# Result tiles turned in 32 by 32 blocks by VectorE, and stored in runs of 128 bytes

## The chip, the cores and the metric

One core of one Trainium2 chip runs the whole program. The time is device microseconds for one execution. Engines named here: TensorE (PE, with its weight loads PEld), VectorE (DVE), ScalarE (ACT), GpSimd (POOL) and SyncE (SP). SyncE does no arithmetic: it issues DMA transfers, one after the other, each once the semaphores that it waits for have come.

## The reference

A residual block on x of 512 tokens by 1024 features, one layer, in float32: a SwiGLU feed-forward network at half weight, a mixer (gated DeltaNet heads and latent attention heads), and a second such network. Each has adaptive layer normalisation from a conditioning vector c.

```
for l in range(DEPTH):
    mod = sc @ w_ada[l] + b_ada[l]
    sh1, s1, g1, sh2, s2, g2, sh3, s3, g3 = jnp.split(mod, N_MOD, axis=-1)
    h = _modulate(x, sh1, s1)
    x = x + 0.5 * g1[:, None, :] * _swiglu(h, ffn1_w_in[l], ffn1_w_out[l])
    h = _modulate(x, sh2, s2)
    y = _hybrid_mixer(h, cos, sin, ...)
    x = x + g2[:, None, :] * y
    h = _modulate(x, sh3, s3)
    x = x + 0.5 * g3[:, None, :] * _swiglu(h, ffn2_w_in[l], ffn2_w_out[l])
return x
```

The change is in how the last x leaves the chip. The output has a row for each token: 1024 floats, 4096 bytes.

## The kernel before

x is kept turned: `self.xT[t]`, t = 0 to 7, is a tile of 128 partitions (features 128t to 128t+127) by 512 columns (tokens). Matrix products are done in three passes of a high and a low part (`mm3`, lines 280 to 282), so that one product of 128 features by 512 tokens is three matmuls.

The second feed-forward network ends in `ffn_pairs`. Its down projection is summed by groups of four blocks of the hidden width; each group updates xT at once. The last group has six blocks. For output tile t, `steps_of(t, a, b, ts)` issues the matmuls of blocks a to b into the PSUM tile `ends[t]`, and `finish(t, ts, p)` (line 990) is VectorE's update: xT[t] becomes p times the gate, plus xT[t]. `close` does this for tiles 0 to 3, whose updates come one behind the other, and returns `leave2`, which ends the kernel with tiles 4 to 7. Tile 7 is done in two halves of 256 tokens, both in one PSUM tile, so that the end has less behind it. A full tile is 18 matmuls.

Each tile of xT must be turned back, since the output has tokens as rows. `store(t, blocks)` does it: for each block of 128 tokens TensorE makes a transpose of 128 by 128 into a PSUM tile (line 731), ScalarE copies the PSUM tile to SBUF (line 733), and SyncE issues one DMA (line 128, the helper `load`) that writes runs of 128 floats, 512 bytes, one for each token. In `leave2` the stores of tiles 0 to 5 go in pairs between the matmuls of tiles 4, 5 and 6 and their updates; that of tile 6 comes between the halves of tile 7; tile 7's own store is in two halves at the very end.

The order of the work in this stretch is the order of the program: `in_order` ties every instruction to the one before it on its engine. Buffers `o` come from a ring of 56 slots of 128 by 512 floats; as many are taken after as before. Two other places of this kernel have operations of the kinds that the change brings in: `base_blocks` (lines 1634 to 1658) sends small matrices through DRAM, in runs of 128 and 64 bytes, some from all 128 partitions and some from 64, and `inverse` (lines 1676 and 1687) makes VectorE transposes in blocks of 32 by 32.

Of the kernel before, what the change touches and what calls it, by code (L numbers as in the profile page):

```python
# [18 lines left out]
P = 128  # L19
# [3 lines left out]
NB = NT // P  # L23
# [66 lines left out]
class Block:  # L90
# [632 lines left out]
            waiting = g  # L723
        next(waiting, None)

    def store(self, t, blocks):
        nc = self.nc
        b0, n = blocks[0], len(blocks)
        p = self.aux()
        for i, b in enumerate(blocks):  # L730
            nc.tensor.transpose(p[:, i * P:(i + 1) * P], self.xT[t][:, b * P:(b + 1) * P], self.ident)
        o = self.slot(s="o")
        nc.scalar.copy(o[:, :n * P], p[:, :n * P])
        self.load(self.out[0][b0 * P:(b0 + n) * P, t * P:(t + 1) * P].rearrange("(b p) n -> p b n", p=P),
                  o[:, :n * P].rearrange("p (b n) -> p b n", b=n))

    def ffn2(self, nb):
        ins = self.ins
# [203 lines left out]
    def ffn_pairs(self, w1, w2, gate, plain, raws, split, accs, side=None):  # L942

        nc = self.nc
        full = slice(0, NT)
        tasks, fill = {}, {}
        add = lambda at, go: tasks.setdefault(at, []).append(go)
        n = FT - plain
# [29 lines left out]
        if side:  # L978
            for i, k in enumerate((0, 4, 1, 5, 2, 6, 3, 7)):
                t = self.token_sums(k % 4, k // 4, True)  # L980
# [8 lines left out]
        def finish(t, ts, p):  # L989
            nc.vector.scalar_tensor_tensor(out=self.xT[t][:, ts], in0=p[:, ts], scalar=gate()[:, t:t + 1],  # L990
                                           in1=self.xT[t][:, ts], op0=ALU.mult, op1=ALU.add)
# [74 lines left out]
        def steps_of(t, a, b, ts=full):  # L1066
            if t not in ends:
                ends[t] = self.aux() if t in ((3, 6, 7) if side else (3,)) else self.acc()
            self.dense(ends[t], units[t][1:], self.act[k0:], ts, a, b, m - 1)
# [3 lines left out]
        for t, s in enumerate((stop, stop + 2, stop + 4, stop + 6)):  # L1073
            add(s, lambda t=t: unit_hi(t))
            add(s + 1, lambda t=t: unit_lo(t))
        last = {stop + 2: (0, 0, 2), stop + 4: (0, 2, 4), stop + 5: (1, 0, 2), stop + 7: (1, 2, 4), stop + 8: (2, 0, 2),
                stop + 10: (2, 2, 4), stop + 11: (0, 4, 5)}
# [72 lines left out]
            return self.norm_half(1, accum, 3)  # L1150

        def leave2():
            for t in range(4, KT - 1):
                steps_of(t, 0, m)
                for e in range(2 * t - 8, min(2 * t - 6, t)):
                    self.store(e, range(NB))
                finish(t, full, ends[t])
            t = KT - 1
            ends[t] = self.acc()
            for half in range(2):  # L1160
                ts = slice(half * HALF, half * HALF + HALF)
                steps_of(t, 0, m, ts)
                finish(t, ts, ends[t])
                if half == 0:
                    self.store(t - 1, range(NB))
                else:
                    self.store(t, range(2))
            self.store(t, range(2, 4))

        return close  # L1170

# [1093 lines left out]
```

## Time and profile before

| | us |
|---|---|
| median of 3 runs | 1039.08 (1038.6 to 1039.15) |
| the profiled execution | 1038.9 |
| its span, first to last instruction | 1037.2 |
| TensorE busy | 1019.9 (98% of the span) |
| VectorE busy | 757.8 (73%) |
| ScalarE busy | 484.2 (47%) |
| DMA, mean over the span | 135 GB/s |

The span is that of one profiled execution; the run takes a little longer than the span. Busy times of TensorE are of pipelined matmuls, so neighbours overlap, and spacing from start to start tells more than the length of one. Times in the rows count from the start of the span. A DMA's row on SPq is the time that its issue takes on SyncE, not that of the transfer. The granted clock of TensorE is 0.999 of full speed over the span.

### The profile page before, as it was taken

To read this page: it belongs to the slowest core of one execution; us is meant where nothing else is said; L and a number is where in the kernel's file an instruction comes from. 1 tells how busy PE (TensorE), PEld (TensorE's weight loads), DVE (VectorE), ACT (ScalarE), POOL (GpSimd) and SP (SyncE) were. 2 spreads that over 40 slices of the span, in tenths; PEclk is the share of its full clock that TensorE was granted. 3 is DMA by queue.
4 is the path that set the end of the run, shared out by engine and by line. 5 is a ranking of instruction groups with operands and counts; after the bars stand their busy time and mean duration, and the time that the engine had idled before them with its cause. 6 is when DMAs were issued, how large, how long until landed. Compare 5 with 4: busy or idle time off the path is not lost.

```text
span 1037.2 us, 17073 instructions
## 1 busy us (share of the span) xinstructions
PE 1019.9 (98%) x6673; PEld 889.2 (86%) x6673; DVE 757.8 (73%) x1416; ACT 484.2 (47%) x865; POOL 114.2 (11%) x232
## 2 busy tenths in 40 slices
PE   7999999999999999999999999999999999999998
PEld 5787878889998999888868778998999999999987
DVE  4467988888887876648977656788778778777642
ACT  4342233255544355649566463565445444444431
POOL 0033331222120101100001111310000000000000
PEclk9999999999999999999999999999999999999999
DMA  9987876778785348511311211163423424323222
GB/s 276 291 269 237 284 225 220 223 191 223 206 216 129 90 106 209 142 41 42 101 41 36 73 42 42 34 150 102 143 82 103 122 82 123 101 82 116 68 61 82
DMA packets 187278, 140.21 MB, mean 135 GB/s; under 512 B 14385, under 2 KB 176190, under 8 KB 187198
## 3 DMA queue, kind: packets, MB, share of 16 engines
q1 hardware_dynamic: 175646, 100.33, 33.9%
q0 software_dynamic: 11552, 38.81, 13.7%
q8 instruction: 52, 0.85, 0.3%
q14 instruction: 28, 0.23, 0.1%
HBM read 127.18 MB, written 2.49 MB: 125 GB/s over the span
## 4 chain that ended last, share of the span: by engine, by line
PE 84%; issue 5%; DVE 4%; ACT 2%; DMA 2%; POOL 1%; SPq 0%; POOLq 0%; DVEq 0%; ACTq 0%
PE pa L280 14%; PE pa L281 13%; PE pa L282 13%; PE pb L916 9%; PE pb L914 9%; PE pb L915 9%; PE pb L280 3%; PE pb L282 2%; PE pb L281 2%; POOL ar L579 1%; PE pb L435 1%; PE pb L1597 1%; DMA wl<-wr 1%; PE pb L1998 1%; PE pb L2028 1%
## 5 line engine op out<-in xcount | busy, mean ns | idle before, releaser
L280 PE MATMUL pa<-ah,wh 128*128 128x512 f32 (+1 forms) x346 | 133.1, 385 | 0.7 <-DVE xT L990 0.5
L281 PE MATMUL pa<-al,wh 128*128 128x512 f32 (+1 forms) x346 | 132.6, 383 | 0.0
L282 PE MATMUL pa<-ah,wl 128*128 128x512 f32 (+1 forms) x346 | 130.9, 378 | 0.2 <-DVE wl L1064 0.2
L280 PE MATMUL pa<-hh,wh 128*128 128x512 f32 (+1 forms) x293 | 110.2, 376 | 0.5 <-ACT hh L482 0.4
L281 PE MATMUL pa<-hl,wh 128*128 128x512 f32 (+1 forms) x293 | 109.2, 373 | 0.6 <-DVE hl L474 0.3
L282 PE MATMUL pa<-hh,wl 128*128 128x512 f32 (+1 forms) x293 | 108.2, 369 | 0.0
L990 DVE SCALAR_TENSOR_TENSOR xT<-pa,mod,xT 128x512 f32<-128x512 f32 (+1 forms) x79 | 57.2, 727 | 37.7 <-PE pa L282 37.7
L579 POOL DMA_DIRECT2D ar<-in_w_ada x112 | 63.4, 635 | 153.3 <-DVE aa L590 46.2
L282 PEld LDWEIGHTS pa<-ah,wl 128*128 128x128 f32 x346 | 65.1, 188 | 13.4 <-DVE wl L1064 0.6
L590 DVE SCALAR_TENSOR_TENSOR aa<-ar,sc,aa 128x512 f32<-128x512 f32 x98 | 73.2, 747 | 2.2 <-DMA ar<-in_w_ada 0.8
L280 PEld LDWEIGHTS pa<-ah,wh 128*128 128x128 f32 x346 | 65.8, 190 | 6.7 <-DVE xT L990 1.1
L281 PEld LDWEIGHTS pa<-al,wh 128*128 128x128 f32 x346 | 65.8, 190 | 5.5 <-DVE al L875 0.2
L280 PEld LDWEIGHTS pa<-hh,wh 128*128 128x128 f32 x293 | 55.3, 189 | 13.0 <-issue 3.4
L208 DVE TENSOR_TENSOR wl<-wr,wh 128x1024 fp32r<-128x1024 f32 (+1 forms) x33 | 38.4, 1164 | 35.7 <-ACT wh L203 35.4
L914 PE MATMUL pb<-fh,wh 128*128 128x256 f32 x224 | 63.4, 283 | 0.5 <-ACT cc L850 0.5
L916 PE MATMUL pb<-hh,wl 128*128 128x256 f32 x224 | 63.4, 283 | 0.2 <-DMA wl<-wr 0.2
L282 PEld LDWEIGHTS pa<-hh,wl 128*128 128x128 f32 x293 | 55.3, 189 | 9.6 <-DVE wl L208 0.4
L281 PEld LDWEIGHTS pa<-hl,wh 128*128 128x128 f32 x293 | 55.3, 189 | 9.3 <-DVE hl L474 1.2
L916 PE MATMUL pb<-fh,wl 128*128 128x256 f32 x224 | 63.3, 283 | 0.0
L915 PE MATMUL pb<-fl,wh 128*128 128x256 f32 x224 | 63.2, 282 | 0.0
L915 PE MATMUL pb<-hl,wh 128*128 128x256 f32 x224 | 63.2, 282 | 0.0
L914 PE MATMUL pb<-hh,wh 128*128 128x256 f32 x224 | 63.2, 282 | 0.0
(448 smaller groups left out, 2793.9 us busy)
## 6 DMA issues: line engine op xcount, KB each, us to landing
wr<-in_ffn_w_in SPq DMA_DIRECT2D x82, 512.0 KB, 3.9
ar<-in_w_ada POOLq DMA_DIRECT2D x112, 256.0 KB, 5.2
wr<-in_ffn_w_out SPq DMA_DIRECT2D x32, 512.0 KB, 5.0
wr<-in_w_in SPq DMA_DIRECT2D x21, 512.0 KB, 3.7
wl<-wr POOLq DMA_DIRECT2D x18, 512.0 KB, 5.7
ar<-in_w_ada SPq DMA_DIRECT2D x16, 512.0 KB, 8.2
wr<-in_ffn_w_out SPq DMA_DIRECT2D x16, 384.0 KB, 4.8
wr<-in_w_out SPq DMA_DIRECT2D x8, 512.0 KB, 3.4
```

What stands on the lines that cost most here:

```text
L208: self.nc.vector.tensor_tensor(out=lo, in0=raw, in1=hi.bitcast(F32), op=ALU.subtract)
L280: mm(out, wh, xh, start=start, stop=False)
L281: mm(out, wh, xl, start=False, stop=False)
L282: mm(out, wl, xh, start=False, stop=stop)
L435: nc.tensor.matmul(pg[32 * q:32 * q + 32, :256], self.sc[:, kc:kc + 1].to_broadcast([P, 32]), a[:, kc], start=(e == 0), stop=(e == 1), til ...
L579: nc.gpsimd.dma_start(tiles[i], a1[kc * P:(kc + 1) * P, o:o + NT])
L590: nc.vector.scalar_tensor_tensor(out=acc, in0=a, scalar=sc, in1=acc, op0=ALU.mult, op1=ALU.add)
L914: mm(out, wh, xh, start=start and k == 0, stop=False, **kw)
L915: mm(out, wh, xl, start=False, stop=False, **kw)
L916: mm(out, wl, xh, start=False, stop=stop and k == 3, **kw)
L990: nc.vector.scalar_tensor_tensor(out=self.xT[t][:, ts], in0=p[:, ts], scalar=gate()[:, t:t + 1], in1=self.xT[t][:, ts], op0=ALU.mult, op1= ...
L1597: nc.tensor.matmul(pa[:, ps], kh[:, ps], x[:, ps], start=True, stop=True)
```

## The change

`store` no longer uses TensorE, PSUM and ScalarE. VectorE transposes the tile (or half tile) in blocks of 32 by 32: within each group of 32 partitions, block j of 32 columns is turned in place. Partition 32i + a of `o` then holds, for each j, feature 32i to 32i + 31 of token 32j + a. So four DMAs are issued, one for each i, each from 32 partitions; they write runs of 32 floats, 128 bytes, 16 runs from each partition for a full tile and 8 for a half. For the last half tile two of the four are issued on ScalarE's queue instead of SyncE's. The stores of tiles 0 to 3 now stand together at the start of `leave2`, each other tile's right behind its update, and there are no transposes left between the matmuls.

```diff
-    def store(self, t, blocks):
-        nc = self.nc
-        b0, n = blocks[0], len(blocks)
-        p = self.aux()
-        for i, b in enumerate(blocks):
-            nc.tensor.transpose(p[:, i * P:(i + 1) * P], self.xT[t][:, b * P:(b + 1) * P], self.ident)
+    def store(self, t, ts, last=False):
+
+        nc = self.nc
+        w = ts.stop - ts.start
         o = self.slot(s="o")
-        nc.scalar.copy(o[:, :n * P], p[:, :n * P])
-        self.load(self.out[0][b0 * P:(b0 + n) * P, t * P:(t + 1) * P].rearrange("(b p) n -> p b n", p=P),
-                  o[:, :n * P].rearrange("p (b n) -> p b n", b=n))
+        nc.vector.transpose(out=o[:, :w], in_=self.xT[t][:, ts])
+        dst = self.out[0][ts, t * P:(t + 1) * P].rearrange("(j a) n -> a j n", a=32)
+        for i in range(4):
+            queue = nc.scalar if last and i % 2 else nc.sync
+            queue.dma_start(dst[:, :, 32 * i:32 * i + 32], o[32 * i:32 * i + 32, :w].rearrange("a (j b) -> a j b", b=32))
...
         def leave2():
+            for e in range(4):
+                self.store(e, full)
             for t in range(4, KT - 1):
                 steps_of(t, 0, m)
-                for e in range(2 * t - 8, min(2 * t - 6, t)):
-                    self.store(e, range(NB))
                 finish(t, full, ends[t])
+                self.store(t, full)
             t = KT - 1
             ends[t] = self.acc()
             for half in range(2):
                 ts = slice(half * HALF, half * HALF + HALF)
                 steps_of(t, 0, m, ts)
                 finish(t, ts, ends[t])
-                if half == 0:
-                    self.store(t - 1, range(NB))
-                else:
-                    self.store(t, range(2))
-            self.store(t, range(2, 4))
+                self.store(t, ts, half == 1)
```

## Rows read from the trace of the kernel before

**Rows 1.** The page, parts 1 and 4: busy time; the chain by engine.
```profile
PE 1019.9 (98%) x6673; PEld 889.2 (86%) x6673; DVE 757.8 (73%) x1416; ACT 484.2 (47%) x865; POOL 114.2 (11%) x232
...
PE 84%; issue 5%; DVE 4%; ACT 2%; DMA 2%; POOL 1%; SPq 0%; POOLq 0%; DVEq 0%; ACTq 0%
```

**Rows 2.** The chain of waits from 1025 us: start, length, what.
```profile
1026.21 0.87 PE pb L731 x8
...
1029.29 0.50 DVE xT L990
...
1029.83 0.39 PE pa L280
...
1032.25 0.23 PE pb L731 x2
...
1032.50 0.38 ACT o L733
...
1032.92 0.42 PE pb L731 x2
...
1033.37 0.37 ACT o L733
```

**Rows 3.** TensorE's timeline, 1011.9 to 1021.1 us: start, length, instruction, idle before.
```profile
1011.92 0.39 PE L280 MATMUL pa<-ah,wh 128*128 128x512 f32 x1
...
1016.01 1.03 PE L731 MATMUL pb<-ident,xT 128*128 128x128 f32 x8
...
1021.03 1.03 PE L731 MATMUL pb<-ident,xT 128*128 128x128 f32 x8
```

**Rows 4.** VectorE's timeline, 1012.9 to 1017 us.
```profile
1012.96 0.74 DVE L990 SCALAR_TENSOR_TENSOR xT<-pb,mod,xT 128x512 f32<-128x512 f32 x1
1016.21 0.75 DVE L990 SCALAR_TENSOR_TENSOR xT<-pa,mod,xT 128x512 f32<-128x512 f32 x1 [2.50 <-PE pa L282]
```

**Rows 5.** VectorE: line 1676 (ns min/median/max); two groups (total us, mean ns).
```profile
L1676 DVE STREAM_TRANSPOSE ti<-ti x4: 311/312/314, 581.5 to 591.1; 128x128 f32<-128x128 f32 x4
...
L875 DVE TENSOR_TENSOR al<-cc,ah 128x512 fp32r<-128x512 f32 x28 | 19.3, 688 | 1.2
...
L869 DVE TENSOR_TENSOR cc<-cc,uc 128x256 f32<-128x256 f32 x28 | 11.7, 418 | 0.0
```

**Rows 6.** SyncE's timeline, DMA issues in six stretches: start, length of issue.
```profile
1.63 3.69 SPq L128 DMA_DIRECT2D xt<-in_x  x8
...
422.28 0.37 SPq L128 DMA_DIRECT2D wr<-in_w_in  x1
...
422.75 0.52 SPq L128 DMA_DIRECT2D wr<-in_w_in  x1
...
552.44 0.37 SPq L1634 DMA_DIRECT2D a_d<-bd  x1
...
555.73 0.63 SPq L1638 DMA_DIRECT2D ba<-a_d  x1
...
556.41 0.67 SPq L1638 DMA_DIRECT2D ba<-a_d  x1
...
1017.25 0.38 SPq L128 DMA_DIRECT2D out_x<-o  x1
...
1017.75 0.44 SPq L128 DMA_DIRECT2D out_x<-o  x1
...
1033.76 0.37 SPq L128 DMA_DIRECT2D out_x<-o  x1
```

**Rows 7.** DMA in 553:555.5, 557:559, 1018:1020.2 us: packets, MB, share; stores' landing.
```profile
q1 hardware_dynamic: 2064, 0.26, 68.8%
...
q1 hardware_dynamic: 2080, 0.13, 69.8%
...
q1 hardware_dynamic: 1056, 0.52, 88.7%
...
out_x<-o SPq DMA_DIRECT2D x7, 256.0 KB, 2.7
```

## The prediction

> **What bounds the kernel now.** I read the page first, then the chain of waits from 1025 us on, then the timelines of TensorE, VectorE and SyncE there. The page says that TensorE is 98% busy and has 84% of the chain that ended last [rows 1]: an instruction taken from TensorE shortens the kernel, and what ScalarE or VectorE do counts only where TensorE or the end waits for it. The chain [rows 2] shows what the change touches: 8 transposes on the path before tiles 5, 6 and 7, then a wait for VectorE between the two halves of the last tile, then a tail of transpose, copy, transpose, copy, and the last store, issued at 1033.76 [rows 6]. The span ends at 1037.2; the profiled run took 1038.9, so 1.7 us lie around the span, and the median of the runs shown, 1039.08, is 0.2 above it. All sums below are against the span.
>
> **TensorE: what goes.** Eighteen matmuls of one tile start at 1011.92 and the next thing starts at 1016.01: 4.09 us. With 8 transposes ahead, tile 5 takes from 1016.01 to 1021.03: 5.02 us [rows 3]. So a group of 8 costs 0.93, the slower first matmuls behind it included. There are three such groups; for the third, ahead of half a tile, I take the 0.87 of the chain [rows 2]: 0.93 + 0.93 + 0.87 = 2.73 us. The four transposes between the halves give nothing: the second half starts at 1029.83 because VectorE's update of the first half ran from 1029.29 for 0.50 [rows 2]; that wait stays and only loses its cover. The last matmul, whose end is where the next transposes start (1032.25), then ends at 1029.5.
>
> **VectorE: what comes.** The rows have a 32 by 32 block transpose of 128x128 in 311 ns. Elementwise operations take 418 ns for 256 columns and 688 for 512, or 1.05 ns a column [rows 5]. The step from 128 to 512 columns is 384 x 1.05 = 0.40, so I take 0.71 for a tile and 0.45 for half a tile. The other end is strict proportion: 4 x 0.311 = 1.24 and 0.62. VectorE has room: it ends tile 3's update at 1012.96 + 0.74 = 1013.7, and the next comes at 1016.21 [rows 4]. Four transposes at 0.71 end at 1016.5 and push tile 4's update by 0.3 us; its PSUM buffer is wanted only by tile 7, at about 1024.3. At 1.24 they would end at 1018.7, still in time. The ScalarE copies go; only the two of the tail were on the path.
>
> **The tail.** Before: from 1032.25 to the issue at 1033.76, 1.51 us. After: update 0.55 with its start, transpose 0.45, wake-up 0.05, so 1.05: the last half is ready for its stores at 1029.5 + 1.05 = 1030.55. From the last store's issue to the end of the span it is 1037.2 - 1033.76 = 3.44 us. In it are 256 runs of 512 B; 1056 packets took 88.7% of 2.2 us on 16 engines, 29.6 ns each, so 256 x 29.6 / 16 = 0.47 us. The new last store has 256 runs of 128 B: the one row with such runs (2064 packets, 68.8% of 2.5 us) gives 13.3 ns [rows 7], so 0.21. That leaves 3.44 - 0.47 + 0.21 = about 3.2 from issue to end.
>
> **Stores: what is moved and multiplied.** Nine stores become 36: 34 on SyncE's queue and 2, of the last half, on ScalarE's. All sixteen of tiles 0 to 3 are now issued together, from about 1013.7 + 0.71 + 0.05 = 1014.5; before, the first store left at 1017.25 [rows 6]. SyncE has nothing else left to issue. Moving data isn't the limit: 2048 runs of a tile at 13.3 ns are 1.7 us on 16 engines, 13.7 us for all eight tiles, with 16 us to do it in. What counts is the spacing c of stores on SyncE, because 32 must be issued ahead of the last half's: 1014.5 + 32c. No row has a store from 32 partitions, so I bound c:
> - Eight loads of x in a row, of 128 runs each, took 3.69 us from the first one's start to the last one's end; less 0.37 for one issue, seven spacings of 0.475 [rows 6].
> - A pair of the present stores, with 512 runs each like the new ones: issues at 1017.25 and 1017.75, the second taking 0.44 where a lone one takes 0.37 [rows 6]. It ended 0.94 after the first one's start. Less its own 0.37, that lets one go every 0.55 to 0.57.
> - A pair of 1024 runs: 422.28 and 422.75, the second 0.52, ended 0.99 after the first's start: 0.62 by the same reckoning.
> - The only three-dimensional transfers on part of the partitions (64), with 1024 runs: 0.63 and 0.67, 0.68 apart and about 0.72 with the second one's gap, though nothing else was in flight. The store of 128-byte runs from all 128 partitions took 0.37 alone [rows 6].
>
> So c lies between 0.475 and 0.72. I take 0.55, that of the pair nearest in runs and direction. The queue then reaches the last half at 1014.5 + 17.6 = 1032.1, later than the 1030.55 at which it is ready. The second of SyncE's two last stores is issued at 1032.65, and the span ends at 1032.65 + 3.2 = 1035.85: a gain of 1.35 us, or 1037.55 in the profiled run's terms, 1037.7 against the median. I say 1037.6. So of the 3 us that TensorE and the tail give, more than half is lost to the issuing queue. In general the end is 1014.5 + 33c + 3.2: equal to before at c = 0.59, 2 us better at 0.53, 2 us worse at 0.65. The two stores on ScalarE's queue have no row; at 0.37 to 0.72 each they are out by 1032.0 and hidden behind SyncE's.
>
> **A rule against it.** The 64-partition reads, in 64-byte runs, took 69.8% of 2 us on 16 engines for 2080 packets: 10.7 ns each, cheaper than the 13.3 ns of a 128-byte run from all partitions [rows 7]; I see no penalty for the narrow span. The Trainium skill, "SBUF — State Buffer", section "Door 1: The DMA port swizzle", says that a transfer on partitions 0 to 31 reaches only 8 of the 16 ports and has little more than half the bandwidth. That speaks against four stores of 32 partitions each. The rows don't bear it out at runs this short, but they hold no store from so few partitions, so it is a rival below.
>
> **Rivals.**
> - *The queue keeps up.* c is 0.475 to 0.5: 32c is 15.2 to 16, the queue is free by 1030.5, and TensorE sets the end: 1030.55 + 0.5 + 3.2 = 1034.25, 2.95 us better: 1036.0. For it: eight issues in a row did 0.475. Against: those had a quarter of the runs.
> - *SyncE's queue overflows; slower.* A transfer on part of the partitions costs what the 64-partition pair cost: c = 0.65 to 0.72, end at 1039.2 to 1041.5, 2.0 to 4.3 us worse: 1041 to 1043.4. It decides from c = 0.59. For it: that pair took 0.63 and 0.67 with idle DMA engines, and is alone in not using all 128 partitions. Against: it had twice the runs and read 64-byte pieces.
> - *The DMA engines become the bound.* Each 128-byte run takes twice 13.3 ns, through eight ports or through writes 4 KB apart: 3.4 us a tile, eight tiles 27.2 from about 1015.4 (0.9 after the first issue, an estimate: of the 2.7 us that a present store of 512 x 29.6 / 16 = 0.95 us takes to land, half the rest), to 1042.6, and 3.44 - 0.87 - 0.47 = 2.1 to the end: 1044.7, 7.5 us worse: 1046.5. For it: no row of 128-byte writes at such a pitch. Against: the present stores, with the same 4 KB pitch, moved at the full pace of 29.6 ns for 512 B.
> - *It doesn't do what it says.* The second half of tile 7 could wait longer, or the stores wait for their buffers: with TensorE's 2.73 us halved, the queue-free end of 1034.25 would be 1035.6: 1037.4. I see no such wait; updates and buffers come in the order of before.
>
> **Chances and range.** About 0.2% of a run is what a measurement here can tell from no change, 2.1 us. Queue limits at c of 0.52 to 0.61, my forecast: 0.42. Queue keeps up: 0.24. Overflow: 0.26. DMA engines: 0.05. The last: 0.03. Of the forecast's 0.42 I put 0.12 beyond 2.1 us better (c near 0.52), so faster by over 0.2% has 0.36; slower has the overflow less a little that stays under 2.1 us worse, plus the DMA case: 0.28; within 0.2%: 0.36. The range reaches from 1035.4 (queue keeps up, with a tail 0.5 us cheaper than summed) to 1042.2 (c = 0.68). The forecast's own range is 1036.2 to 1039.5.
>
> **What would show it.** TensorE: no gap or transpose between tiles 4, 5, 6 and 7, eighteen matmuls every 4.1 us, the last matmul ending near 1029.5, and a bare wait of 0.5 us between the halves. VectorE: block transposes of 0.71 and 0.45. SyncE: 34 issues, back to back from 1014.5 to past 1032, and that the last half's first issue starts well after its transpose has ended. The issue spacing is the number to read first: 0.475, 0.55 or 0.7 tells the cases apart. Packets of 128 B should take 13 ns; at 25 the DMA case holds. The prediction is wrong at its root if TensorE's end does not move by 2.5 to 3 us, and wrong in size if c is not near 0.55.

## The result, and the profile after

The changed kernel takes 1046.01 us (median of 4 runs, 1045.85 to 1046.35), the kernel before 1039.12 in the same comparison: a ratio of 1.0066, 95% interval 1.0055 to 1.0078. It is 6.9 us slower. I had forecast 1037.6, with a range to 1042.2. The profiled execution has a span of 1044.2 against 1037.2.

TensorE did what was forecast. Its timeline, against [rows 3]: tile 4 begins at 1012.13 (1011.92 before, so this trace runs 0.2 us behind), tile 5 at 1016.21, tile 6 at 1020.29, 4.08 us apart, with no transposes between them. At 1027.26 the second half of tile 7 starts, after a bare wait of 0.58.

```profile
1012.13 0.39 PE L280 MATMUL pa<-ah,wh 128*128 128x512 f32 x1
...
1016.21 0.39 PE L280 MATMUL pa<-ah,wh 128*128 128x512 f32 x1
...
1020.29 0.39 PE L280 MATMUL pa<-ah,wh 128*128 128x512 f32 x1
...
1027.26 0.39 PE L280 MATMUL pa<-ah,wh 128*128 128x256 f32 x1 [0.58 <-DVE xT L990]
```

VectorE's transposes took what I had put in, 0.71 for a tile and 0.45 for a half (line 731, against the 311 ns of [rows 5]); the last one ends at 1030.67.

```profile
1013.82 2.48 DVE L731 STREAM_TRANSPOSE o<-xT 128x512 f32<-128x512 f32 x4
1016.41 0.75 DVE L990 SCALAR_TENSOR_TENSOR xT<-pa,mod,xT 128x512 f32<-128x512 f32 x1
1017.19 0.71 DVE L731 STREAM_TRANSPOSE o<-xT 128x512 f32<-128x512 f32 x1
...
1030.22 0.45 DVE L731 STREAM_TRANSPOSE o<-xT 128x256 f32<-128x256 f32 x1
```

From 1030.7 no engine computes any more, and yet the span lasts to 1044.2. Where that time went is in the waits of SyncE's queue (us in total, times, longest; the 17.2 us are the idle time before the first store), and in the issues around it, SyncE's on SPq and ScalarE's on ACTq:

```profile
SPq L735 <- DVE o L731: 17.2, 1, 17.2
SPq L735 <- DMA out_x<-o: 8.0, 1, 8.0
```

```profile
1014.55 0.36 SPq L735 DMA_DIRECT2D out_x<-o  x1
...
1017.13 1.74 SPq L735 DMA_DIRECT2D out_x<-o  x1
...
1023.29 1.05 SPq L735 DMA_DIRECT2D out_x<-o  x2
...
1023.84 8.84 SPq L735 DMA_DIRECT2D out_x<-o  x2
...
1030.70 0.88 ACTq L735 DMA_DIRECT2D out_x<-o  x2
...
1032.36 0.32 SPq L735 DMA_DIRECT2D out_x<-o  x1
...
1040.83 0.89 SPq L735 DMA_DIRECT2D out_x<-o  x2
```

SyncE issues the 16 stores of tiles 0 to 3 from 1014.55 to 1024.34 and then stands still until 1032.36, although tile 4 was turned at 1017.9. It waits for a store (DMA out_x) to land. It goes on 1.66 us after ScalarE's first store, of the last half, was issued at 1030.70. Only then do the 18 stores of tiles 4 to 7 follow, the last at 1041.28. The stretches show the DMA engines (last two columns: share, GB/s) idle in the meantime. The column before these two is TensorE's granted clock, a share of full speed; it is 0.50, the lower of its two levels (1.2 GHz), in the last stretch, where the engine has had nothing to do since 1029.7, and costs nothing there.

```profile
1023.00:1025.00 2.00, 2.00 (x13) 1.75 (x12) 0.43 (x1) 0.00 (x0) 0.00 (x0) 1.00 0.79 117
1025.00:1027.00 2.00, 1.68 (x15) 1.48 (x13) 1.31 (x3) 0.00 (x0) 0.00 (x0) 1.00 0.18 27
1027.00:1029.00 2.00, 1.74 (x14) 1.74 (x15) 0.65 (x2) 0.00 (x0) 0.00 (x0) 1.00 0.00 0
1029.00:1031.00 2.00, 0.67 (x6) 0.46 (x4) 0.93 (x2) 0.00 (x0) 0.00 (x0) 1.00 0.00 0
...
1033.00:1035.00 2.00, 0.00 (x0) 0.00 (x0) 0.00 (x0) 0.00 (x0) 0.00 (x0) 0.50 0.72 107
```

The row of SyncE's queue in the DMA view, 1014 to 1044.2 us, answers to [rows 7]: 16416 packets in 45.8% of 30.2 us on 16 engines are 13.5 ns each, as forecast.

```profile
q1 hardware_dynamic: 16416, 2.03, 45.8%
```

The built program says which store is waited for. In this program a DMA signals that it has landed by raising one of eight completion semaphores (counters that a queue can wait on); which one is fixed when the program is built. Both queues draw from the same eight, in turn, and each DMA waits for the last user of the semaphore that it takes. A listing of the built kernels, with the number of the semaphore waited for, which is also the one taken:

```
changed: SyncE   tile 2, stores 1 to 4     7, 0, 2, 4
         SyncE   tile 3, stores 1 to 4     5, 6, 7, 0
         SyncE   tile 4, stores 1 to 4     1, 2, 3, 4
         ScalarE last half, both stores    1, 3
all on SyncE: tile 2: 7, 0, 1, 2   tile 3: 3, 4, 5, 6   tile 4: 7, 0, 1, 2
```

ScalarE's two stores, the last to be ready, have been dealt numbers 1 and 3 in the middle of tile 2's turn; why the build places them there stays open. The next to get number 1 is the first store of tile 4. So a store that is ready at 1017.9 waits for one that cannot be issued before 1030.7. The trace's landing marks agree: semaphore 1 is raised for tile 0's third store by 1017.48, then not again until ScalarE's first store lands, from 1032.13 to 1032.30, and SyncE issues at 1032.36.

### The profile page after: what moved, and what is told of

Read it like the earlier page. It is cut to its first block, busy times and chain, and to the rows that moved or that the text cites. A ratio compares the mean times of both kernels' runs of the same rounds, so it can differ in the third digit from the quotient of the medians.

```text
span 1044.2 us, 17040 instructions
## 1 busy us (share of the span) xinstructions
PE 1016.0 (97%) x6641; PEld 886.1 (85%) x6641; DVE 763.1 (73%) x1425; ACT 480.9 (46%) x856; POOL 114.9 (11%) x232
## 4 chain that ended last, share of the span: by engine, by line
PE 89%; DVE 4%; ACT 2%; DMA 1%; issue 1%; SPq 0%; POOL 0%; POOLq 0%; DVEq 0%; ACTq 0%
PE pa L280 15%; PE pa L281 14%; PE pa L282 14%; PE pb L914 8%; PE pb L915 8%; PE pb L916 8%; PE pb L280 4%; PE pb L282 4%; PE pb L281 4%; DMA ar<-in_w_ada 1%; PE pb L435 1%; PE pb L1594 1%; PE pb L1995 1%; PE pb L2025 1%; PE pb L1998 0%
## 5 line engine op out<-in xcount | busy, mean ns | idle before, releaser
L282 PEld LDWEIGHTS pa<-ah,wl 128*128 128x128 f32 x346 | 65.1, 188 | 13.3 <-DVE wl L1064 0.6
```

Of the source, the lines that this page charges most:

```text
L282: mm(out, wl, xh, start=False, stop=stop)
```

## The experiments

Theory 1 is this wait. Theory 2 is that a queue or ring was full after so many stores and had to drain. A third, ScalarE's stores being slow in themselves, is already weak: they were issued in 0.38 and 0.46 us.

**All on SyncE.**

```diff
-            queue = nc.scalar if last and i % 2 else nc.sync
+            queue = nc.sync
```

> All 36 stores on SyncE, none on ScalarE. Theory 1 (ScalarE's two stores carry completion semaphores that SyncE's stores of tile 4 wait for, so that SyncE stands still for 8.0 us): the wait is gone, SyncE issues without a break. In the changed kernel's trace the first 16 issues took from 1014.55 to 1024.34; sixteen more at 0.55 (the four halves at 0.50) end at 1032.9, the last half's fourth is issued at 1034.4, and 2.9 us later (1041.28 to 1044.2 in that trace) the span ends: 1037.3, a run of 1039.0, against 1039.1 before and 1046.0 changed. Theory 2 (SyncE's queue or the rings of the DMA engines are full after some 18 stores and must drain): a stand still of about 8 us stays, 1046 or more.

Measured: 1038.94 us, ratio 1.0001 to before (0.9992 to 1.001). The wait for a DMA is gone from SyncE's list; 36 stores are issued from 1014.24 to 1034.39, and the span ends at 1036.8.

```profile
SPq L735 <- DVE o L731: 17.2, 1, 17.2
SPq L2258 <- DMA out_x<-o: 0.7, 2, 0.4
```

```profile
1014.24 0.36 SPq L735 DMA_DIRECT2D out_x<-o  x1
...
1016.81 1.51 SPq L735 DMA_DIRECT2D out_x<-o  x1
...
1033.94 0.45 SPq L735 DMA_DIRECT2D out_x<-o  x1
```

The two stores that were to relieve SyncE cost 7 us. Without them the change is worth nothing: what TensorE and the tail give, the issuing takes.

**Ordered.** The two stores stay on ScalarE; a scheduling order alone, without a wait, puts them behind SyncE's stores, so that they are dealt semaphores 0 and 2 behind these.

```diff
-            queue.dma_start(...)
+            ins = queue.dma_start(...).ins
+            if queue is nc.sync:
+                self.synced = ins.name
+            else:
+                self.follow(ins, self.synced)
```

> The same stores on the same queues as in the changed kernel; only the order in which the program hands out completion semaphores differs: ScalarE's two stores take theirs after SyncE's. Theory 1: the wait of 8.0 us is gone; SyncE gets to the last half at 1032.9, issues its two by 1033.4, and the span ends 2.9 us later at 1036.3: a run of 1038.0. Theory 2, or ScalarE's stores being slow by themselves: 1046 as changed.

Measured: 1038.57 us, ratio 0.9995 (0.9987 to 1.0004). The wait for another store is gone from SyncE's list of its issues (the 1.0 us of line 2262 is at the kernel's end), with the same stores on the same queues. This run settles it: in the two built programs every engine has the same instructions in the same order, and only the dealing of semaphores differs.

```profile
SPq L735 <- DVE o L731: 17.2, 1, 17.2
SPq L2262 <- DMA out_x<-o: 1.0, 1, 1.0
```

```profile
1014.09 0.36 SPq L735 DMA_DIRECT2D out_x<-o  x1
...
1017.22 1.71 SPq L735 DMA_DIRECT2D out_x<-o  x1
...
1032.57 0.40 SPq L735 DMA_DIRECT2D out_x<-o  x1
```

SyncE reaches the last half at 1032.57; my forecast had 1032.1.

**Four on ScalarE.** The wait should move, and grow.

```diff
-            queue = nc.scalar if last and i % 2 else nc.sync
+            queue = nc.scalar if last else nc.sync
```

> All four stores of the last half on ScalarE, unordered as in the changed kernel. Their completion semaphores are taken earlier in the round of eight, and the first SyncE store that takes one of these again is now the third of tile 3 instead of the first of tile 4. Theory 1: SyncE stands still two issues earlier, from about 1023.2, until ScalarE's first store has landed at 1032.4, some 9.1 us; then 14 stores at 0.55 and four at 0.50 follow, the last one issued at 1041.5, the end 2.9 later: 1044.4, a run of 1046.2. If the stop came from the number of stores in flight or from a full ring, it would come at the same store as in the changed kernel, and ScalarE's taking of the last two would make the run 1 us shorter: 1045.0.

Measured: 1046.2 us, ratio 1.0067 (1.0052 to 1.0082). SyncE stops after 14 stores instead of 16, at 1022.13, and goes on at 1031.35, when ScalarE's first store, issued at 1029.73, has landed. (This trace runs 1.0 us ahead of the changed kernel's.)

```profile
SPq L735 <- DMA out_x<-o: 9.2, 1, 9.2
```

```profile
1021.62 0.50 SPq L735 DMA_DIRECT2D out_x<-o  x1
...
1029.73 1.89 ACTq L735 DMA_DIRECT2D out_x<-o  x4
...
1031.35 0.32 SPq L735 DMA_DIRECT2D out_x<-o  x1
```

The place and the length are those of theory 1; a full ring would not have stopped two stores earlier.

**One transfer for a tile.** What TensorE and the tail are worth when issuing is cheap.

```diff
-        dst = self.out[0][ts, t * P:(t + 1) * P].rearrange("(j a) n -> a j n", a=32)
-        for i in range(4):
...
+        self.load(self.out[0][ts, t * P:(t + 1) * P].rearrange("(b p) n -> p b n", p=P),
+                  o[:, :w].rearrange("p (b n) -> p b n", n=P))
```

> VectorE's block transposes stay, but each tile (or half) is stored by one transfer from all 128 partitions in runs of 512 bytes, as in the kernel before; the 32 by 32 blocks then land in wrong places of the output, which this kernel leaves so. It shows what TensorE and the tail give when the queue costs nothing. My sum: last half ready at 1030.7, issued at once, 3.4 us to the end (1033.76 to 1037.2 before): 1034.1, a run of 1035.9, 3.2 us better than before. If TensorE's 2.7 us were lost elsewhere: 1038 to 1039.

Measured: 1034.65 us, ratio 0.9961 (0.9947 to 0.9974): 4.2 us better than before, and 1.2 us less than the sum's 1035.9. The last store is issued at 1030.02 and the span ends at 1032.8, some 2.8 later, where I had put 3.4 from the kernel before. The other 0.7 is that this profile's end of computing is ahead of the changed kernel's (last transpose done at 1030.0 against 1030.67). The two kernels compute the same up to there; such profiles lie up to 1.0 us apart, as that of four on ScalarE does.

```profile
1029.55 0.45 DVE L731 STREAM_TRANSPOSE o<-xT 128x256 f32<-128x256 f32 x1
```

```profile
1030.02 0.37 SPq L128 DMA_DIRECT2D out_x<-o  x1
```

**Both queues for every tile.**

```diff
-            queue = nc.scalar if last and i % 2 else nc.sync
+            queue = nc.scalar if i % 2 else nc.sync
```

> Of every tile's four stores two are on SyncE and two on ScalarE, so the completion semaphores come in the order in which the stores are issued. Theory 1 with one issue cost for each queue: 16 stores a queue ahead of the last half, 0.55 apart, keep up with TensorE; the last half is issued from 1030.7, the span ends at 1030.7 + 0.5 + 2.9 = 1034.1, a run of 1035.9, 3.2 us better than before. If both queues share one generator, so that stores come 0.55 apart over both: as with all on SyncE, 1039. Theory 2 (the rings are full): 1044 or more.

Measured: 1036.01 us, ratio 0.9976 (0.9967 to 0.9984). The semaphores are now dealt as the stores are issued; waits on them fall to 1.5 us in three. Four stores of the last half leave together at 1030.17, two a queue:

```profile
1030.17 0.32 SPq L735 DMA_DIRECT2D out_x<-o  x1
...
1030.17 0.38 ACTq L735 DMA_DIRECT2D out_x<-o  x1
...
1030.53 0.45 SPq L735 DMA_DIRECT2D out_x<-o  x1
```

The queues' rows (1014 to 1037 us) give 64.3% of 23 us on 16 engines for 16960 packets, 14.0 ns. The 24 stores of tiles 0 to 5 are issued from 1014.02 to 1024.17, 0.42 us each over both queues, faster than the 0.55 of one. From 1016 to 1026 us the DMA engines are full (share 0.99 to 1.04), and an issue takes up to 1.2 us: there the data set the pace, and no longer the issues. Behind 1026 us the engines have room again.

```profile
q10 hardware_dynamic: 8480, 1.05, 33.2%
q1 hardware_dynamic: 8480, 1.05, 31.1%
```

```profile
1016.00:1018.00 2.00, 2.00 (x11) 1.65 (x10) 1.34 (x2) 0.00 (x0) 0.00 (x0) 1.00 1.01 146
...
1024.00:1026.00 2.00, 2.00 (x19) 1.95 (x17) 1.46 (x2) 0.00 (x0) 0.00 (x0) 1.00 0.99 145
...
1028.00:1030.00 2.00, 1.14 (x10) 0.93 (x8) 0.79 (x2) 0.00 (x0) 0.00 (x0) 1.00 0.65 91
```

**Early stores.** All on SyncE, tiles 0 to 3 each right behind its update.

```diff
                 finish(t, ts, ends[t])
+                if not side:
+                    self.store(t, full)
...
-            for e in range(4):
-                self.store(e, full)
```

> All stores on SyncE; those of tiles 0 to 3 are made right behind each tile's update instead of behind tile 3's, so that the queue starts at about 1011.8 instead of 1014.5. If the spacing of the issues is what bound the kernel with all stores on SyncE: 32 issues and the one long issue of about 1.1 extra us end at 1030.4, before the last half is ready at 1030.7; its four issues and 2.9 us end at 1035.1, a run of 1036.8 against 1038.9. If the landing of the data bound it: 1038.9. The long issue (1.5 to 1.7 us, the sixth or seventh in the kernels so far): if it comes with the number of issues it is again the sixth or seventh, near 1015; if it comes with a moment, near 1017, about the tenth.

Measured: 1036.5 us, ratio 0.9977 (0.9968 to 0.9985). The queue starts at 1011.40 and is ready at 1029.7, before the last half, whose first store leaves at 1030.28. So with all on SyncE it was the spacing of the issues that bound, and 2.8 us of earlier start buys 2.4 us of end (1036.5 against 1038.9). The long issue is now the twelfth, and again near 1017:

```profile
1011.40 0.36 SPq L735 DMA_DIRECT2D out_x<-o  x1
...
1016.73 2.08 SPq L735 DMA_DIRECT2D out_x<-o  x2
...
1030.28 0.32 SPq L735 DMA_DIRECT2D out_x<-o  x1
```

**Two PSUM tiles.** Both queues as above, and each half of tile 7 in its own PSUM tile, taken from the ring `aux` that the transposes used before. The cut shows the second edit alone.

```diff
-            ends[t] = self.acc()
             for half in range(2):
+                ends[t] = self.aux()
```

> As with two stores of each tile on either queue, and the two halves of tile 7 in two PSUM tiles instead of one. If the wait between the halves (0.5 us of VectorE's update, which the transposes had covered) is a wait for the PSUM tile and lies bare on the path, TensorE runs on and the end comes 0.5 to 0.6 us earlier: 1035.4 against 1036.0. If something else sets it, 1036.0.

Measured: 1035.29 us, ratio 0.996 (0.9948 to 0.9972), 0.7 less than with one tile. From tile 7's first matmul to the end of the last transpose it is 5.48 us, against 6.30 in the kernel with one tile (1024.38 to 1029.86, and 1023.84 to 1030.14). The chain with one tile goes through VectorE's update of the first half; with two it runs through the halves without a wait for VectorE until the last update. This is the fastest of the kernels that store every value in its place, 3.8 us better than before.

```profile
1026.19 0.49 DVE xT L990
...
1026.73 0.39 PE pa L280
```

```profile
1026.58 0.12 PE pb L282
1026.69 0.12 PE pb L280
...
1028.73 0.13 PE pb L282
...
1028.89 0.49 DVE xT L990
...
1029.41 0.45 DVE o L731
```

## Why the prediction was wrong, by its steps

- **TensorE, right.** 2.73 us, ending at 1029.5: it ended at 1029.68 in a trace 0.2 behind, 2.77 us earlier. The four transposes between the halves gave nothing, and the wait they covered lay bare; giving each half a PSUM tile of its own won it back.
- **VectorE and the tail up to the stores, right.** 0.71 and 0.45; last half ready at 1030.55 forecast, 1030.70 measured.
- **The spacing c, right.** I took 0.55 from the pair of old stores [rows 6]. From one tile to the next the four issues take 2.2 us: 0.55. The dearer end, 0.72 from the transfers on 64 partitions, was not seen. I missed the one issue of 1.5 to 1.7 us. With the wait taken away (the ordered kernel) the span ends at 1036.3, where the forecast had 1035.85, and the run takes 1038.57 against 1037.6. One slip in the range: by the prediction's own sum c = 0.68 gives 1042.0 against the median, not 1042.2; nothing hangs on it.
- **The two stores on ScalarE's queue: this step failed.** I wrote that they "are out by 1032.0 and hidden behind SyncE's". I costed their issue, and it was cheap (0.38 and 0.46), but not the semaphores that they take. They were a wait added, for the first store of tile 4 with 17 others queued behind it on SyncE: 8.0 us, and 1046.0 instead of the 1038.6 of the ordered kernel. The last rival, which weighs waits of the stores, names updates and buffers, not the semaphores.
- **The rivals.** The DMA rival's time, 1046.5, met the measured 1046.0 by accident: its packets of twice 13.3 ns were 13.5 ns. The chip's answer is in the rows, not in the total. The overflow, by the spacing of 64-partition transfers, did not come.
- **The rule against it.** The four stores from 32 partitions moved 128 bytes in 13.5 ns on one queue and 14.0 on two, against the 13.3 of all 128 partitions [rows 7]. The Trainium skill, "SBUF — State Buffer", "Door 1: The DMA port swizzle", gives 32 partitions little more than half the bandwidth of 128, 189 GB/s against 328 in transfers of 1 MiB. The runs show no loss, but they don't test this rule: they moved about 147 GB/s, less than its figure for 32 partitions, and stores from all four groups of partitions were in flight together.
- **Two queues.** SyncE alone took 20.2 us for 36 stores, and a second queue made the run 2.9 us shorter. The Trainium skill, "DMA: Bandwidth & Descriptors", "Issuing engines are not separate DMA queues", says that issuing from several engines saves only the sequencer's time, usually small beside the transfer. The trace agrees on what is saved; here, with a spacing of 0.55 us against 512 x 13.5 / 16 = 0.43 us of data, it was not small.

## What to carry to other kernels

When a change multiplies DMAs or puts some on another queue, follow not only the queue and the data but the completion semaphores: list for each DMA which earlier one it waits for. A late DMA on an idle queue can be dealt a semaphore early, and then holds up a whole queue of ready ones; give it an order behind them, or split every tile alike over the queues. And price a train of DMAs by the spacing of a back-to-back pair with as many runs each, not by one issue alone.

## What the runs showed that I had not expected

One issue in each train on SyncE alone, or on SyncE but for the last half, took 1.5 to 1.7 us instead of 0.5: the sixth or seventh store, but the twelfth when the train began 2.2 to 3.2 us earlier. So it comes with a moment, not with a number of stores. In that stretch (1016.5 to 1018.5 us of the changed kernel) the DMA view has one packet of the instruction queue, 3.8% of 2 us on 16 engines, 1.2 us on one of them:

```profile
q8 instruction: 1, 0.02, 3.8%
```

In the early kernel it is 3.9% of 2.5 us, 1.6, between 1016.5 and 1019. The landing marks point the same way. Each store raises its semaphore sixteen times; of the two in flight at that moment in the changed kernel, fifteen marks had come by 1018.01 and 1018.58, the sixteenth only at 1019.73 and 1020.07. That the train waits for the one DMA engine that loads instructions fits all this, but no run took that load away; it stays open.
